# A planner for TensorE's tiles and a VectorE-GpSimd exclusion, a new order of parts, and key products of two heads in turn, in a hybrid encoder block

## Chip, cores and metric

One core of a Trainium2 chip runs the whole kernel. The metric is device time in microseconds (us), from the start of the execution to its end on that core; lower is better.

## What is computed

One layer of an encoder over 512 tokens of width 1024: `x <- LayerNorm(alpha*x + Mixer(x))`, then `x <- LayerNorm(alpha*x + HierMoE(x))`. All matrix work is in float32 or in a split of float32 into two parts. The change touches the mixer, which is, in short:

```python
h = jnp.einsum('btd,de->bte', x, w_in)
(q_na, k_na, v_na, q_dn, k_dn, v_dn, z_dn, b_f, b_b, a_f, a_b, gate_na, gate_dn) = jnp.split(h, offs, axis=-1)
y_na = neighborhood_attention(q_na, k_na, v_na, na_rpb) @ w_proj_na
y_dn = gated_deltanet_bidir(q_dn, k_dn, v_dn, z_dn, ...) @ w_proj_dn
merged = jax.nn.sigmoid(gate_na) * y_na + jax.nn.sigmoid(gate_dn) * y_dn
return merged @ w_out
```

Neighbourhood attention has 8 heads of 64. The gated DeltaNet has 8 heads of 64 and two directions; for each it forms the products of keys with keys and queries, solves a triangular system for each chunk, and scans the chunks with a state of 64 x 64 for each head.

```python
kk = jnp.einsum('bhnid,bhnjd->bhnij', kb, k) * decay
sol = lax.linalg.triangular_solve(a_mat, rhs, left_side=True, lower=True, unit_diagonal=True)
intra = jnp.einsum('bhnid,bhnjd->bhnij', q, k) * decay
def step(S, xs):
    v_new = u_c - jnp.einsum('bhik,bhkv->bhiv', w_c, S)
    o = jnp.einsum('bhik,bhkv->bhiv', qe, S) + jnp.einsum('bhij,bhjv->bhiv', a_c, v_new)
    S = S * jnp.exp(gl)[..., None, None] + jnp.einsum('bhik,bhiv->bhkv', ke, v_new)
```

## The kernel before

The program has three stretches. The first, the mixer with the first LayerNorm and the router, is recorded and then ordered by a planner (`Plan`): each operation goes into a list with its engine (V is VectorE, DVE in the profile; S is ScalarE, ACT; G is GpSimd, POOL; PE is TensorE; Y is the DMA queue of SyncE, SP), a cost from `Plan.cost`, and the operations that it must follow. `Plan.emit` ranks each operation by the longest chain of costs behind it, plays the engines forward with these costs, takes the best-ranked operation that can start, and writes the instructions out in that order. Each engine then runs its own instructions strictly in that order. The second stretch is the mixture of experts (written out by hand, 17 rounds), the third the last LayerNorm, ordered by the same planner.

What the mixer is made of, by the names that appear in the rows:

- `dense` makes one 128-column slice of `h`: 8 pieces of weights are loaded (`wraw`), split into two parts (ACT writes `whi`, POOL `wlo`), and 24 matmuls of 512 columns (`mm<-xhi,whi`, `mm<-xlo,whi`, `mm<-xhi,wlo`) add up in PSUM. There are 44 such slices and one narrow one. They wait for little and serve as filler for everything else. `K`, `Q` and `V` slices feed the DeltaNet and pass a convolution on DVE (`cy`), `Z` slices its output gate, `G` slices the 16 merge gates, and `q` and `v` steps make the slices of neighbourhood attention.
- `D` steps (`delta_step`) are the DeltaNet of four heads, `D00` to `D03` for the first four and `D10` to `D13` for the others. `products` makes the decay (`psp<-Gh,mfr`, `E`) and the key products: four matmuls per call, in each 64 rows of one head against 256 columns (`psp<-kqv`), whose results go through the one PSUM buffer `psp` and are multiplied by `E` on DVE into `NA`. There are 8 calls. `solve` inverts a triangular matrix by doubling: for each of 6 levels four short matmuls (`ps<-RR,N` or `ps<-RR,NT`), a copy to SBUF (`ylv`, on DVE or ACT), eight short matmuls (`ps<-ylv,RR`, `ps<-RR,ylv`) and an update (`RR`, on DVE or ACT). `scan` carries the state on (`vn`, `S`, `O`), and `rms` ends the four heads (`osq`, `zs`).
- `s` steps (`na_scores`) and `o` steps (`na_out`) are the attention of two heads: 8 score matmuls with 64 rows (`psn<-kqv`, 64 or 128 columns), softmax on DVE, ACT and POOL, transposes (`psn<-con,sb`), and 8 output matmuls, each of 64 output rows (`psn<-PT,kqv`). There are 64 of each kind in all.

A matmul with 64 rows or 64 output rows uses half of TensorE's 128 x 128 array, and the instruction says which half. In the profile such a matmul has the form `64*128`, `128*64` or `64*64`, all others `128*128`; a float32 matmul appears as two MATMUL rows, so `x2` is one of them.

`SEQ` lists the parts in the order in which they are recorded. Ties of rank and the order in which PSUM and SBUF buffers are given out follow it. `+a4`, `+b6` and `+d6` open buffers for gates, `+c -c` and `+n -n` the work space of the convolution and of attention.

The planner before costs a matmul by its columns alone, plus a weight load when the matmul ahead is too short to hide it; it knows no cost for going from the full array to half of it and back, and it lets DVE and POOL run side by side at all times.

Of the kernel before, what the change touches and what calls it, by code (L numbers as in the profile page):

```python
# [9 lines left out]
F32 = mybir.dt.float32  # L10
# [67 lines left out]
"""  # L78


# [3 lines left out]

NORM1 = "VGV VGV VGV VGV VVG VVG SGV SVG".split()
NORM2 = "VSGG QD QSGG QPS QSGV QSGV QPS QD A B A B".split()


class Ref:
# [73 lines left out]


class Op:
    __slots__ = ("eng", "call", "args", "kw", "cost", "pred", "succ", "rank", "bytes", "pool", "prio", "cover", "at")

    def __init__(self, eng, call=None, args=(), kw=None):
        self.eng, self.call, self.args, self.kw = eng, call, args, kw or {}
        self.cost, self.pred, self.succ, self.rank, self.bytes, self.pool = 0.0, set(), [], 0.0, 0, None  # L170
        self.prio = self.cover = self.at = 0.0


class Stack:
# [16 lines left out]
class Plan:  # L191
# [57 lines left out]
    def record(self, eng, name, args, kw):  # L249
        op = Op(eng, name, args, kw)  # L250
        op.prio = self.prio
        out = [kw["out"]] if "out" in kw else [args[0]]
        out += [kw["accum_out"]] if "accum_out" in kw else []
        refs = [(r, False) for r in list(args) + list(kw.values()) if isinstance(r, Ref) and not any(r is o for o in out)]
        refs += [(r, True) for r in out if isinstance(r, Ref)]
        for r, wr in refs:
            t = r.tile
            box = (0, 127, 0, t.size) if t.pool.psum else r.box()
            for o, b in t.writes + (t.reads if wr else []):
                if o is not op and b[0] <= box[1] and box[0] <= b[1] and b[2] <= box[3] and box[2] <= b[3]:  # L260
# [17 lines left out]
        return op  # L278

    def cost(self, eng, name, args, kw, out):  # L280
        if eng == "Y":
# [3 lines left out]
        if eng == "PE":  # L285
            dt = args[1].view.dtype
            if name == "transpose":
                return 0.003 + max(args[1].shape[0], 64) * (2 if dt == F32 else 1) / 2400
            if dt == F32:
                return 0.003 + max(4 * n / 2400, 0.16)  # L290
            return 0.003 + max(n, 64) / 2400
        if name in ("tensor_reduce", "bn_stats"):
            return 0.07 + int(np.prod(args[1].shape[1:])) / 960
        if name == "reciprocal":
            return 0.07 + n / 160
        psum = any(r.tile.pool.psum for r in ins)
        if eng == "S":
            extra = 0.09 * sum(isinstance(kw.get(k), Ref) for k in ("bias", "scale", "accum_out"))
            return (0.05 if psum else 0.09) + n / 1200 + extra
        if eng == "G":  # L300
            if name == "memset":
                return 0.035 + n / 1200
            if name == "affine_select":
                return 0.06 + n / 960
            return 0.15 + n / (480 if ins[-1].view.dtype == F32 and len(ins) > 2 else 600)
        if self.ptr and name in ("tensor_scalar", "scalar_tensor_tensor"):
            n += 58 * sum(isinstance(r, Ref) for r in args[2:4 if name == "tensor_scalar" else 3])
        fast = not psum and (all(r.view.dtype == F16 for r in ins) or len(ins) == 2)
        return 0.07 + n / (1920 if fast else 960)

    def emit(self, wait=WAIT, trace=True):
# [20 lines left out]
            if not left[o]:  # L332
                cand[o.eng].append(o)
        order, dma, self.when = [], 0.0, []
        pe = 1.0

        def start(o):
            if o.eng == "PE":
                load = 0.03 if o.args[1].view.dtype == F16 else 0.107
                return max(free["PE"] + max(0.0, load - pe), est[o])  # L340
            return max(free[o.eng], est[o])

        for _ in range(len(ops)):
            best = None
            for k, c in cand.items():
                if not c:
                    continue
                m = min(max(free[k], est[o]) for o in c) + wait.get(k, 0)
                if k == "PE":
                    o = max((o for o in c if est[o] <= m),  # L350
                            key=lambda o: o.rank + o.prio - LAM * max(0.0, LOADT[o.args[1].view.dtype == F16] - pe))
                else:
                    o = max((o for o in c if est[o] <= m), key=lambda o: o.rank + o.prio)
# [6 lines left out]
            if o.eng is not None:  # L360
                free[o.eng] = end
            if o.eng == "PE":
                pe = o.cover
# [59 lines left out]
def encoder_block(ctx, tc, aps, out):  # L423
# [4 lines left out]
    pool = plan.pool  # L428
# [274 lines left out]
    def products(gr, t):  # L703
# [4 lines left out]
            NAs.append(un.tile([128, 2, 4, 128], F32, name="NAl" if late else "NA", bufs=3 if late else 2))  # L708
        kq = KQT[gr]
        tt = slice(t * 128, t * 128 + 128)  # L710
        for h in range(2):
            kp = ps([128, 2, 2, 128], tag="p")
            r = slice(h * 64, h * 64 + 64)
            for p in range(2):
                PE.matmul(kp[:, p], kq[r, p, 0, tt], kq[r, p, :, tt], start=True, stop=True,
                          skip_group_check=True)
            for d in range(2):
                V.tensor_tensor(NAs[d][:, :, h::2], kp.rearrange("p a q i -> p q a i"),
                                Es[d][:, None, h::2].to_broadcast([128, 2, 2, 128]), op=OP.mult)
        return NAs  # L720

# [1178 lines left out]
```

## Time and profile before

| | us |
|---|---|
| median of 3 runs | 981.56 |
| lowest, highest | 974.43, 985.82 |
| profiled execution, whole | 980.33 |
| its span, first to last instruction | 978.5 |
| TensorE busy in the span | 919.2 |
| VectorE busy | 529.9 |
| GpSimd busy | 361.6 |
| ScalarE busy | 357.3 |

The profiled execution took 1.8 us more than its span and stands 1.2 us under the median. Busy time of PE is the union of modelled pipeline times: a PE that is busy all the time need not be issuing at its peak, so the starts of its rows say more than their lengths. The mixer up to the output projections takes the first half of the span (its first projection starts at 515.7 us), the rest of the planned stretch goes to about 640 us, the experts to about 965 us.

### The profile page before, as it was taken

How to read it: one execution, taken by the hardware profiler on the slowest of the kernel's cores; microseconds unless marked ns; L12 is line 12 of the kernel's file. 1: busy time of each engine (PE TensorE's matmuls, PEld its weight loads, DVE VectorE, ACT ScalarE, POOL GpSimd, SP SyncE). 2: the span in 40 equal slices, each digit the busy share in tenths (PEclk: the TensorE clock that was granted, in tenths of full speed). 3: DMA queues.
4: the chain of work that ended last, by engine and by line, in shares of the span. 5: the costliest groups of instructions: out<-in, count | busy, mean ns of one | idle time of the engine just before them, and what ended most of it. 6: DMA issues, size and time to landing. Idle time of an engine off the chain costs nothing. (4 is left out here: it accounts for less than half of the span.)

```text
span 978.5 us, 15388 instructions
## 1 busy us (share of the span) xinstructions
PE 919.2 (94%) x5667; PEld 593.4 (61%) x5667; DVE 529.9 (54%) x1181; ACT 357.3 (37%) x925; POOL 361.6 (37%) x500
## 2 busy tenths in 40 slices
PE   7899989999999999999999999779999999999995
PEld 5666766776677666677788789753343343343432
DVE  5889887649743352330322337844455454455447
ACT  5455554435645564444353321202112121121114
POOL 5766446447545433444556742410000000001003
PEclk9999979999999999999999999889999999999997
DMA  6220000121021221111246455949998999999402
GB/s 238 66 65 22 24 22 23 45 70 44 23 66 44 71 72 44 49 45 44 86 172 222 145 222 208 381 179 330 344 344 308 374 357 357 324 378 368 185 1 86
DMA packets 39965, 157.71 MB, mean 161 GB/s; under 512 B 5786, under 2 KB 6042, under 8 KB 29008
## 3 DMA queue, kind: packets, MB, share of 16 engines
q1 hardware_dynamic: 37584, 152.81, 43.3%
q0 software_dynamic: 2304, 3.90, 1.2%
q8 instruction: 45, 0.74, 0.3%
q14 instruction: 32, 0.26, 0.1%
HBM read 156.99 MB, written 4.19 MB: 165 GB/s over the span
## 5 line engine op out<-in xcount | busy, mean ns | idle before, releaser
L392 POOL TENSOR_TENSOR wlo<-wraw,whi 128x256 fp32r<-128x256 f32 (+1 forms) x220 | 162.9, 753 | 169.1 <-ACT whi L392 114.6
L392 PE MATMUL mm<-xhi,whi 128*128 128x512 f32 (+1 forms) x360 | 142.9, 431 | 13.8 <-ACT whi L392 4.8
L392 PE MATMUL mm<-xhi,wlo 128*128 128x512 f32 (+1 forms) x360 | 142.0, 426 | 0.0
L392 PE MATMUL mm<-xlo,whi 128*128 128x512 f32 (+1 forms) x360 | 140.8, 424 | 0.0
L1591 PE MATMUL hp<-wu,xT 128*64 128x512 f32 x544 | 137.4, 607 | 0.0
L1565 DVE TENSOR_TENSOR xn<-xn,gat 128x512 f32<-128x512 f32 x128 | 86.6, 686 | 89.0 <-PE gat L1563 89.0
L392 ACT CAST whi<-wraw 128x256 fp32r<-128x256 f32 (+1 forms) x228 | 87.4, 405 | 129.5 <-PE mm L392 83.9
L1563 PE MATMUL gat<-part,hot 128*128 128x512 f32 x256 | 92.8, 444 | 0.0
L392 PEld LDWEIGHTS mm<-xhi,whi 128*128 128x128 f32 (+1 forms) x360 | 66.8, 192 | 33.0 <-issue 9.8
L1563 PEld LDWEIGHTS gat<-part,hot 128*128 128x128 f32 x256 | 38.4, 189 | 66.6 <-issue 51.9
L392 PEld LDWEIGHTS mm<-xlo,whi 128*128 128x128 f32 (+1 forms) x360 | 67.0, 191 | 13.5 <-issue 3.2
L392 PEld LDWEIGHTS mm<-xhi,wlo 128*128 128x128 f32 (+1 forms) x360 | 67.0, 191 | 13.4 <-issue 3.5
L1597 ACT ACTIVATE hid<-hp 128x256 f32<-128x256 f32 x17 | 6.5, 385 | 175.3 <-PE hp L1591 175.3
L1591 PEld LDWEIGHTS hp<-wu,xT 128*64 128x64 f32 x544 | 31.7, 135 | 60.3 <-issue 58.0
L1612 PE MATMUL yp<-wu,hid 128*64 128x512 f32 x272 | 62.1, 598 | 0.5 <-ACT hid L1606 0.5
L1577 POOL TENSOR_TENSOR cw<-ic 128x1 f32<-128x1 f32 x17 | 3.2, 187 | 150.3 <-ACT ic L1515 140.7
L392 DVE TENSOR_TENSOR RR<-RR,ps 128x512 f16<-128x512 f16 x64 | 43.1, 682 | 28.7 <-PE ps L392 28.5
L1538 POOL DMA_INDIRECT xg<-x1d,ix x16 | 16.9, 1053 | 111.1 <-DVE oh L1527 92.4
L1556 DVE TENSOR_TENSOR part<-yp,part 128x512 fp32r<-128x512 f32 x34 | 23.4, 692 | 37.0 <-ACT part L1555 37.0
L392 DVE TENSOR_TENSOR ylv<-ps,mlv 128x256 f16<-128x256 f32 x64 | 26.6, 419 | 29.6 <-PE ps L392 29.3
L1612 PEld LDWEIGHTS yp<-wu,hid 128*64 128x64 f32 x272 | 18.0, 136 | 35.8 <-issue 28.8
L1555 ACT CAST part<-yp 128x512 fp32r<-128x512 f32 x34 | 19.8, 586 | 46.7 <-PE yp L1612 45.5
(373 smaller groups left out, 1792.4 us busy)
## 6 DMA issues: line engine op xcount, KB each, us to landing
wu<-in_wgu SPq DMA_DIRECT2D x54, 1024.0 KB, 6.7
wu<-in_wdn SPq DMA_DIRECT2D x28, 1024.0 KB, 6.5
wraw<-in_wT SPq DMA_DIRECT2D x42, 512.0 KB, 3.4
wu<-in_wgu SPq DMA_DIRECT2D x56, 256.0 KB, 5.6
wu<-in_wdn SPq DMA_DIRECT2D x24, 256.0 KB, 5.9
wraw<-in_wp SPq DMA_DIRECT2D x8, 512.0 KB, 3.6
wraw<-in_wo SPq DMA_DIRECT2D x8, 512.0 KB, 3.6
kqv<-in_rpb SPq DMA_DIRECT2D x4, 640.0 KB, 3.9
```

The source lines that it names most:

```text
L392: getattr(self.eng[o.eng], o.call)(*[f(v) for v in o.args], **{k: f(v) for k, v in o.kw.items()})
L1538: G.indirect_dma_start(out=dst, out_offset=None, in_=x1d, in_offset=bass.IndirectOffsetOnAxis(ap=ix, axis=0), bounds_check=T - 1, oob_is_e ...
L1555: S.copy(part[:, c], yps[c])
L1556: V.tensor_tensor(part[:, 2 + c], yps[c], part[:, c].bitcast(F32), op=OP.subtract)
L1563: PE.matmul(sm_, hot[:, t * 128:t * 128 + 128], part[:, 2 * i + h], start=i == 0, stop=i == 1)
L1565: V.tensor_tensor(v, v, sm_, op=OP.add)
L1577: G.tensor_tensor(cw[j], ic[j][:, 0:1], ic[j][:, 1:2], op=OP.add)
L1591: PE.matmul(hp[rows2[h]], xT[:, k, rows2[h]], gw(j, h, k), start=k == 0, stop=k == KC - 1, skip_group_check=True)
L1597: S.activation(hid, hp[:, 0:256], AF.Tanh, scale=0.5)
L1612: PE.matmul(y[rows2[h]], hT[:, f, rows2[h]], dw(j, h, f, c), start=f == 0, stop=f == 1, skip_group_check=True)
```

## The change

Six edits: five in what orders the mixer, one in how it issues a product.

1. `SEQ` has another order of parts: the first value slice and a `Z` slice come ahead, `Q` slices come earlier, all four `Z` slices and four gates stand among the DeltaNet's parts in other places, `D10` comes ahead of the end of the convolutions' work space, the steps of attention among `D11` to `D13` change places, and 7 gates instead of 6 stand behind `+d6`.
2. The planner models TensorE by a class `Array`: the mode (which part of the array), a group (which half), a weight load per group that is not hidden behind the same group, two parts for a float32 matmul, and 0.095 us (`DRAIN`) for each change of mode.
3. The choice among ready PE operations is by rank minus `LAM` (10, was 20) times the time that the array would stand still for it.
4. Operations of POOL and those of DVE that read and write SBUF alone exclude each other in the planner (`port`).
5. An operation of PE that follows one of PE may start when that one starts.
6. `products` takes two PSUM buffers, `psn` for one half's heads and `ps0` for the other's, and issues the four matmuls in turn between the halves; before it issued both of one half, then both of the other, through `psp`.

```diff
 WAIT = {"PE": 0.05, "V": 0.1, "S": 0.1, "G": 0.2, "Y": 0.0, None: 0.0}
-LAM = 20.0
-LOADT = (0.107, 0.03)
+LAM = 10.0
+DRAIN = 0.095
 SEQ = """
-+a4 +c K00 Q00 V00 K01 Q01 V01 D00 K10 K11 D01 Q10 Q11 Z0 D02 V10 V11 Z1 G G G G D03 Z2 Z3 -c +n D10
-q0 v0 s00 s01 q1 o00 o01 v1 s10 s11 D11 q2 o10 o11 v2 s20 s21 D12 q3 o20 o21 v3 s30 s31 D13 o30 o31
--n +b6 G G G G G G -m +d6 G G G G G G
++a4 +c V00 K00 Z0 Q00 K01 Q10 Q01 V01 D00 K10 D01 Z1 Q11 D02 K11 V11 G V10 G G D03 D10 G Z2 Z3 -c +n
+q0 s00 v0 s01 o00 o01 q1 v1 s11 s10 D11 q2 o10 o11 v2 s21 o21 D12 s20 o20 q3 v3 s30 s31 D13 o30 o31
+-n +b6 G G G G G -m +d6 G G G G G G G
 """
+class Array:
...
+    def run(self, o, est, commit=False):
+        mode, group, load, part, parts = o.array
+        issue, f, tk = self.issue, 0.0, 0.0
+        if mode == self.mode:
+            f, tk = self.free.get(group, 0.0), self.taken.get(group, 0.0)
+        elif self.mode is not None:
+            issue = max(issue, self.end() + DRAIN)
+        first = None
+        for _ in range(parts):
+            st = max(max(issue, tk, est) + load, f, issue + 0.007)
+            first = st if first is None else first
+            issue = tk = st
+            f = st + part
...
+        op.port = eng == "G" or eng == "V" and self.shared(name, args, kw, out[0])
         if eng == "PE":
-            op.cover = int(np.prod(out[0].shape[1:])) / (1200 if args[1].view.dtype == F32 else 2400)
+            op.array = self.array(name, args)
+            op.cost = op.array[4] * max(op.array[2], op.array[3])
...
         def start(o):
             if o.eng == "PE":
-                load = 0.03 if o.args[1].view.dtype == F16 else 0.107
-                return max(free["PE"] + max(0.0, load - pe), est[o])
-            return max(free[o.eng], est[o])
+                return pe.run(o, est[o])[0]
+            s = max(free[o.eng], est[o])
+            if o.port:
+                s = max(s, port["V" if o.eng == "G" else "G"])
+            return s
+
+        def gain(o):
+            return o.rank + o.prio - LAM * (pe.run(o, est[o])[0] - max(pe.end(), est[o]))
...
-                est[q] = max(est[q], end + self.lat(o, q))
+                est[q] = max(est[q], s if o.eng == q.eng == "PE" else end + self.lat(o, q))
...
+        kp = [ps([128, 2, 2, 128], tag="n0"[h]) for h in range(2)]
+        for p in range(2):
+            for h in range(2):
+                r = slice(h * 64, h * 64 + 64)
+                PE.matmul(kp[h][:, p], kq[r, p, 0, tt], kq[r, p, :, tt], start=True, stop=True,
+                          skip_group_check=True)
         for h in range(2):
-            kp = ps([128, 2, 2, 128], tag="p")
-            r = slice(h * 64, h * 64 + 64)
-            for p in range(2):
-                PE.matmul(kp[:, p], kq[r, p, 0, tt], kq[r, p, :, tt], start=True, stop=True,
-                          skip_group_check=True)
```

The instructions are the same in kind and number on each engine; their order changes on all of them. Three places show it.

On PE, in the output of attention (`psn<-PT,kqv`), before, between dense matmuls (`mm`):

```order
L392 MATMUL mm<-xhi,whi 128x512 x2
L392 MATMUL mm<-xlo,whi 128x512 x2
L392 MATMUL psn<-PT,kqv 64x128
L392 MATMUL mm<-xhi,wlo 128x512 x2
L392 MATMUL psn<-PT,kqv 64x128
L392 MATMUL mm<-xhi,whi 128x512 x2
L392 MATMUL psn<-PT,kqv 64x128
```

The same place now, the first output matmuls of the same two heads:

```order
L447 MATMUL mm<-xhi,whi 128x512
L447 MATMUL mm<-xlo,whi 128x512 x2
L447 MATMUL mm<-xhi,wlo 128x512
L447 MATMUL mm<-xhi,whi 128x512
L447 MATMUL mm<-xhi,wlo 128x512
L447 MATMUL mm<-xlo,whi 128x512
L447 MATMUL psn<-PT,kqv 64x128 x8
```

The eight output matmuls, which stood one by one between pairs of dense ones, stand together.

On PE, the key products of the last four heads (`psp<-kqv 128x256`, before), among dense and score matmuls:

```order
L392 MATMUL mm<-xlo,whi 128x512
L392 MATMUL mm<-xhi,wlo 128x512
L392 MATMUL mm<-xhi,whi 128x512
L392 MATMUL psp<-kqv 128x256
L392 MATMUL mm<-xlo,whi 128x512
L392 MATMUL psn<-kqv 128x128
L392 MATMUL mm<-xhi,wlo 128x512
L392 MATMUL psn<-kqv 128x128 x2
L392 MATMUL psp<-kqv 128x256
```

The key products of the last four heads now, where `psn` holds one half's and `ps_2852` the other's:

```order
L447 MATMUL mm<-xlo,whi 128x512
L447 MATMUL pss<-vn,NAl 128x64 x4
L447 MATMUL psn<-kqv 128x256
L447 MATMUL ps_2852<-kqv 128x256
L447 MATMUL psn<-kqv 128x256
L447 MATMUL ps_2852<-kqv 128x256
L447 MATMUL pss<-S_327,kqv 128x128 x4
```

One call of the four now stands in one piece and in turn between the halves; in the first four heads the two halves of a call still stand apart for the most part, two matmuls at one place and two at another.

On SP, the loads of the dense slices' weights (`wraw<-in_wT`) and of attention's bias (`kqv<-in_rpb`, one ahead of each pair of heads), before:

```order
L392 DMA conb<-in_conb 128x1280
L392 DMA wraw<-in_wT 128x1024 x17
L392 DMA kqv<-in_rpb 128x1280
L392 DMA wraw<-in_wT 128x1024 x8
L392 DMA kqv<-in_rpb 128x1280
L392 DMA wraw<-in_wT 128x1024 x4
L392 DMA kqv<-in_rpb 128x1280
L392 DMA wraw<-in_wT 128x1024 x3
L392 DMA kqv<-in_rpb 128x1280
L392 DMA wraw<-in_wT 128x1024 x10
```

The same loads now:

```order
L447 DMA conb<-in_conb 128x1280
L447 DMA wraw<-in_wT 128x1024 x23
L447 DMA kqv<-in_rpb 128x1280
L447 DMA wraw<-in_wT 128x1024 x3
L447 DMA kqv<-in_rpb 128x1280
L447 DMA wraw<-in_wT 128x1024 x2
L447 DMA kqv<-in_rpb 128x1280
L447 DMA wraw<-in_wT 128x1024 x4
L447 DMA kqv<-in_rpb 128x1280
L447 DMA wraw<-in_wT 128x1024 x10
```

Six slices have moved from between the bias loads to ahead of the first one (23 and 17), so 9 stand between the four bias loads where 15 stood.

## Rows read from the trace of the kernel before

**Rows 1.** The page, part 2: busy tenths in 40 equal slices of the span.
```profile
PE   7899989999999999999999999779999999999995
PEclk9999979999999999999999999889999999999997
```

**Rows 2.** Stretches: length; PE, PEld, DVE, ACT, POOL busy us (instructions); clock; DMA; GB/s.
```profile
45.00:300.00 255.00, 235.89 (x2059) 179.40 (x2059) 188.72 (x394) 127.24 (x329) 141.71 (x186) 0.96 0.13 42
300.00:470.00 170.00, 169.09 (x1094) 116.85 (x1093) 55.12 (x143) 86.61 (x255) 75.26 (x118) 1.00 0.16 54
```

**Rows 3.** Timeline, PE, attention's output: start us, us, engine, line, operation, tiles, form, xcount.
```profile
326.07 0.43 PE L392 MATMUL psn<-PT,kqv 128*64 128x128 f32 x2
326.43 0.73 PE L392 MATMUL mm<-xhi,wlo 128*128 128x512 f32 x2
327.10 0.43 PE L392 MATMUL psn<-PT,kqv 128*64 128x128 f32 x2
```

**Rows 4.** Timeline, PE, dense matmuls alone, late in the mixer.
```profile
493.84 0.62 PE L392 MATMUL mm<-xlo,whi 128*128 128x512 f32 x2
494.30 0.62 PE L392 MATMUL mm<-xhi,wlo 128*128 128x512 f32 x2
```

**Rows 5.** Timeline, PE, six output matmuls that stand together.
```profile
441.34 1.38 PE L392 MATMUL psn<-PT,kqv 128*64 128x128 f32 x12
442.65 0.88 PE L392 MATMUL pss<-x,NAl 128*128 128x64 f32 x6
```

**Rows 6.** Timeline, PE, key products: one matmul, then two of the same half.
```profile
87.96 0.70 PE L392 MATMUL psp<-kqv 64*128 64x256 f32 x2
88.59 0.29 PE L392 MATMUL ps<-ylv,RR 128*128 128x64 f16 x4
...
90.62 1.13 PE L392 MATMUL psp<-kqv 64*128 64x256 f32 x4
91.68 0.29 PE L392 MATMUL ps<-RR,N 128*128 128x64 f16 x4
```

**Rows 7.** The page, part 5: key products on their way through DVE.
```profile
L392 DVE TENSOR_TENSOR NA<-psp,E 128x512 f32<-128x512 f32 x20 | 13.5, 686 | 5.0 <-PE psp L392 4.1 <-PE pss L392 0.9
```

**Rows 8.** Timeline, PE and DVE, one level of a solve.
```profile
165.04 0.28 PE L392 MATMUL ps<-RR,ylv 128*128 128x64 f16 x4
...
165.36 0.69 DVE L392 TENSOR_TENSOR RR<-RR,ps 128x512 f16<-128x512 f16 x1
...
166.43 0.29 PE L392 MATMUL ps<-RR,NT 128*128 128x64 f16 x4
...
166.75 0.42 DVE L392 TENSOR_TENSOR ylv<-ps,mlv 128x256 f16<-128x256 f32 x1
...
167.56 0.29 PE L392 MATMUL ps<-ylv,RR 128*128 128x64 f16 x4
```

**Rows 9.** Timeline, PE, a stretch of the first four heads without dense matmuls (those between left out).
```profile
120.20 0.39 PE L392 MATMUL mm<-xhi,wlo 128*128 128x512 f32 x1
...
128.60 1.22 PE L392 MATMUL psp<-kqv 64*128 64x256 f32 x2 [0.38 <-ACT E L392]
...
134.30 0.77 PE L392 MATMUL mm<-xhi,whi 128*128 128x512 f32 x1
```

**Rows 10.** The four stretches up to 300 us at clock 0.50: the longest, their sum.
```profile
127.80:138.00 10.20, 9.29 (x69) 6.06 (x68) 6.91 (x17) 3.44 (x11) 4.08 (x6) 0.50 0.17 51
...
sum 20.40, PE 19.50 PEld 14.11 DVE 13.62 ACT 6.75 POOL 10.14; mean PE 4.87 PEld 3.53 DVE 3.41 ACT 1.69 POOL 2.53
```

**Rows 11.** Instructions by tile (min/median/max ns, first and last start): solve, scan and end of the DeltaNet.
```profile
L392 ACT COPY NT<-psp x16: 1002/1012/1039, 75.4 to 351.3; 128x1024 f16<-128x1024 f16 x16
L392 ACT COPY vn<-pss x16: 358/373/413, 103.5 to 464.0; 128x256 f32<-128x256 f32 x16
L392 ACT COPY vn<-pss x4: 372/373/375, 181.8 to 205.5; 128x256 f32<-128x256 f32 x4
L392 DVE SCALAR_TENSOR_TENSOR zs<-pss,nw,zs x4: 742/748/750, 230.9 to 493.1; 128x512 f32<-128x512 f32 x4
```

More of the change, by code (lines that the diff above doesn't have):

```diff
@@ L86, with __init__, end @@
 NORM2 = "VSGG QD QSGG QPS QSGV QSGV QPS QD A B A B".split()
+class Array:
+    def __init__(self):
+        self.mode, self.free, self.taken, self.issue = None, {}, {}, 0.0
+    def end(self):
+        return max(self.free.values(), default=0.0)
+    def run(self, o, est, commit=False):
[11 more added lines that the diff above has]
+            f = st + part
+        if commit:
+            if mode != self.mode:
+                self.mode, self.free, self.taken = mode, {}, {}
+            self.free[group], self.taken[group], self.issue = f, tk, issue
+        return first, f
 class Ref:
@@ L165 @@
 class Op:
-    __slots__ = ("eng", "call", "args", "kw", "cost", "pred", "succ", "rank", "bytes", "pool", "prio", "cover", "at")
+    __slots__ = ("eng", "call", "args", "kw", "cost", "pred", "succ", "rank", "bytes", "pool", "prio", "array", "at", "port")
     def __init__(self, eng, call=None, args=(), kw=None):
@@ L170, in __init__ @@
         self.cost, self.pred, self.succ, self.rank, self.bytes, self.pool = 0.0, set(), [], 0.0, 0, None
-        self.prio = self.cover = self.at = 0.0
+        self.prio = self.at = 0.0
+        self.array, self.port = None, False
 class Stack:
@@ L278, in record, with shared, array @@
         return op
+    def shared(self, name, args, kw, out):
+        ins = [r for r in list(args[1:]) + list(kw.values()) if isinstance(r, Ref) and int(np.prod(r.shape[1:])) > 1]
+        ins = [r for r in ins if r is not out]
+        if out.tile.pool.psum or any(r.tile.pool.psum for r in ins):
+            return False
+        if name in ("tensor_tensor", "scalar_tensor_tensor"):
+            return True
+        return name in ("tensor_scalar", "tensor_copy", "memset")
+    def array(self, name, args):
+        out, w = args[0], args[1]
+        n = int(np.prod((args[2] if name != "transpose" else out).shape[1:]))
+        K, M = w.shape[0], int(np.prod(w.shape[1:]))
+        size = [32 if x <= 32 else 64 if x <= 64 else 128 for x in (K, M)]
+        at = (w.box()[0] // size[0] if size[0] < 128 else 0, out.box()[0] // size[1] if size[1] < 128 else 0)
+        dt = w.view.dtype
+        load = M * (1 if dt == F16 else 4) / 4800
+        if name == "transpose":
+            return tuple(size), at, load, n / 2400, 1
+        if dt == F32:
+            return tuple(size), at, load, n / 1200, 2
+        return tuple(size), at, load, n / 2400 + (0.005 if dt == F16 else 0.01), 1
     def cost(self, eng, name, args, kw, out):
-        if eng == "Y":
+        if eng in ("Y", "PE"):
             return 0.06
@@ L284, in cost @@
         ins = [r for r in list(args) + list(kw.values()) if isinstance(r, Ref)]
[L285 to L291, printed above, removed]
         if name in ("tensor_reduce", "bn_stats"):
@@ L334, in emit @@
         order, dma, self.when = [], 0.0, []
-        pe = 1.0
+        pe, port = Array(), {"V": 0.0, "G": 0.0}
         def start(o):
             if o.eng == "PE":
-                load = 0.03 if o.args[1].view.dtype == F16 else 0.107
-                return max(free["PE"] + max(0.0, load - pe), est[o])
-            return max(free[o.eng], est[o])
+                return pe.run(o, est[o])[0]
[5 more added lines that the diff above has]
+            return o.rank + o.prio - LAM * (pe.run(o, est[o])[0] - max(pe.end(), est[o]))
         for _ in range(len(ops)):
@@ L348, in emit @@
                 m = min(max(free[k], est[o]) for o in c) + wait.get(k, 0)
[L349 to L353, printed above, removed]
+                o = max((o for o in c if est[o] <= m), key=gain if k == "PE" else lambda o: o.rank + o.prio)
                 s = start(o)
@@ L359, in emit @@
             end = s + o.cost
-            if o.eng is not None:
+            if o.eng == "PE":
+                s, end = pe.run(o, est[o], True)
+                free["PE"] = pe.issue
+            elif o.eng is not None:
                 free[o.eng] = end
-            if o.eng == "PE":
-                pe = o.cover
+            if o.port:
+                port[o.eng] = end
             if o.eng == "Y" and o.call != "none":
@@ L710, in products @@
         tt = slice(t * 128, t * 128 + 128)
[L711 to L716 removed]
+        kp = [ps([128, 2, 2, 128], tag="n0"[h]) for h in range(2)]
[4 more added lines that the diff above has]
+                          skip_group_check=True)
+        for h in range(2):
             for d in range(2):
[L718 removed]
+                V.tensor_tensor(NAs[d][:, :, h::2], kp[h].rearrange("p a q i -> p q a i"),
                                 Es[d][:, None, h::2].to_broadcast([128, 2, 2, 128]), op=OP.mult)
```

## The prediction

> **What bounds the kernel now.** I read the slices first, then the stretches, then the timeline of TensorE (PE) inside them. The slices [rows 1] show PE at 9 tenths or more almost everywhere, with dips at the very start, in slices two to five and near the router. The stretches [rows 2] divide the mixer: from 45 to 300 us, where the DeltaNet of the first four heads runs, PE is busy 235.89 of 255 us, so 19.1 us idle, while DVE is busy 188.72 (74%). From 300 to 470 us, where attention and the other four heads run, PE is busy 169.09 of 170, and DVE only 55.12. So in the second stretch what PE issues sets the time, in the first one partly what it waits for. The change leaves the instructions of every engine as they are, and the experts' code too; PE is busy there nearly throughout. I cost the experts, projections and LayerNorms at nothing: they follow the mixer and should only shift.
>
> In the second stretch busy does not mean useful. In the timeline [rows 3] a single output matmul of attention starts at 326.07, the next at 327.10, with two dense matmuls between: 1.03 us. Two dense matmuls alone take 0.46 us [rows 4]. So one output matmul costs 0.57 us, of which 0.36 lies between its start and the next dense one (326.07 to 326.43) and 0.21 in the neighbours' starts. Six that stand together take 1.31 us from start to successor [rows 5], with the same 0.21 around them 1.52, or 0.25 each. The difference of 0.32 us is what leaving the full array, coming back, and loading weights that nothing hides costs.
>
> **Output matmuls.** By my count of the order, the 64 stood in 60 pieces: 57 of one, two of two, one of three; without full-array work between them that makes 58 visits. At 56 singles x 0.57 plus 0.6 and 1.5 for the two longer visits this is 34.0 us. Now there are 15 visits: 8 of five to eight matmuls (55 in all, 13.8 us at 0.25), 2 of two (0.57 each, one in each half), 5 of one (2.9): 17.8 us. Gain 16 us, nearly all in the stretch where PE is full, so on the path. Bounds: 8 us, if grouped matmuls gained half of what rows 5 show; 20, if eight in a row cost less than six.
>
> **Key products.** One matmul takes 0.63 us to its successor (87.96 to 88.59), two of one half 1.06 (90.62 to 91.68) [rows 6]; with 0.21 around, 0.84 and 1.27. Before: 16 singles and 8 twos, 23.6 us. Four in turn between halves are not in the trace; the bounds are 1.27 (the halves run fully beside each other) and 2.3 (one after the other). I take 1.27, because the six of rows 5, which also alternate, took 1.31 and not six times a single's 0.36. But the order shows that only 3 of 8 calls got both halves together; the others remain 7 twos, one three and 3 singles. That makes 11 x 1.27 + 3 x 0.84 = 16.5 us: gain 7. The bounds are 3 and 10.
>
> Here a rule speaks against the change. DVE takes 686 ns for each half and direction of a call [rows 7], 2.7 us per call, twice the 1.27 that PE would need. The Trainium skill, "TensorEngine Tiling (Array Packing)", section "PSUM Bottleneck", says that tiling speeds up TensorE but not the evacuation of PSUM, which may then bound. By that the 7 us would be nothing for the solve behind the products. In the second stretch PE has other work meanwhile and DVE is busy a third of the time, so what PE saves counts; I keep the 7.
>
> **Scores and transposes.** The 64 score matmuls stood in 37 visits and stand in 14. At 0.21 around each visit 23 fewer save 4.8 us; now and then three of the same half follow each other, so I take 4 (bounds 0 and 7). Half-width transposes: 1 us (0 and 2). Sum of the regrouping: 16 + 7 + 4 + 1 = 28 us.
>
> **The solves.** One level is two hops. After the last short matmul is issued (three steps of 0.03 us behind 165.04), the update RR runs from 165.36 to 166.05; after that of 166.43, `ylv` runs from 166.75 to 167.17 [rows 8]. With a tenth for the start on PE, PE needs other work for about 1.05 and 0.75 us. I counted in both orders the PE work that stands in these places, at the spacing of rows (0.23 us a dense matmul, 0.03 a short one): of 176 places, 62 hold too little before and 25 now, and what lacks adds up to 11.8 and 5.0 us. Gain 7 us. Bounds: 0, as DVE may be late for other reasons (its 74%), and 19, all the idle time of the first stretch. New PSUM buffers can delay as well: `ps0` also serves the solves of one direction, `psn` the convolutions' transposes, so a product waits for them and they for its two multiplications by E on DVE (2 x 0.69 us); the idle time of PE in the first four heads covers this, as three of these four calls were split because of it.
>
> **The clock.** Four stretches up to 300 us run at clock 0.50, 1.2 instead of 2.4 GHz, 20.4 us in sum [rows 10]; the longest follows a stretch in which PE had only the solves' short matmuls and waits [rows 9], and a key product took 1.22 us there instead of 0.70. At most half of 20.4, 10 us, comes back; I take 3, and 10 in either direction as bounds, since the new order can have its own dips.
>
> **What is moved to where.** Six dense slices are now loaded, and issued, ahead of attention: 6 x 24 x 0.23 = 33 us of filler leave the second stretch for the first. That helps the solves above and starves what comes later. Before, one bare stretch of 115 matmuls lasted from 120.43 to 134.30 [rows 9], where their own steps come to about 6 us: 8 lost, partly by the clock. Now five bare stretches of 50 to 107 matmuls, 353 in all, lie in the second stretch. At the same rate they would lose 25 us, 17 more than now. But attention has longer and independent matmuls there (0.25 us, not 0.03), so I charge 5 (bounds 0 and 17).
>
> **Sum.** 28 + 7 + 3 - 5 = 33 us. The profiled execution took 980.33 us, so 947; it stands 1.2 under the median of 981.56, on whose scale I say 948 us.
>
> **Rivals.**
> A. *The first stretch heals.* If the moved filler takes all of PE's idle time and the clock stays up, the gain is 28 + 19 + 10 = 57: 924 us. For it: the starved places fall to less than half. Against: DVE's 74% does not change.
> B. *Only attention gains.* PE waits on DVE in the first stretch however it is ordered, so the gain there (about 5 of the 7 for key products, the solves, the clock) is nothing, and the bare stretches cost 12: 16 + 2 + 5 - 12 = 11, 970 us. For it: the split calls, and the bare stretches in the order.
> C. *The DeltaNet ends too late (slower).* The last transposes of a solve now have 544 matmuls, 268 of them dense, between them and the first projection; before 791 and 411. At 0.23 us and some 0.08 for the others that is 84 us of work. The chain through solve, scans and `rms` needs 28 us from the first solve's copy (75.4) to its first scan (103.5), 3 scans of 7.9 (181.8 to 205.5), and 29 from the last scan (464.0) to the last `zs` (493.1), 81 in sum; before it took 142 (351.3 to 493.1) [rows 11]. If it still takes 142, PE waits 58: 980 - 33 + 58 = 1005 us on the profiled scale, 1006 on the median's. It decides from 84 + 33 = 117 us on.
> D. *It does not do what it says.* If halves do not run beside each other in the longer groups, outputs and key products give 11, not 23: 960 us.
>
> **Chances.** The forecast 0.56, A 0.14, B 0.14, D 0.06, no change to be told (gains given back to bare stretches, clock and PSUM waits, about 977) 0.05, C 0.05. A difference of 1%, 10 us, is about what a measurement of this kernel can tell from no change; 971.7 is that bound. B lies at it, so half of it and a little of the forecast's tail (0.01) count as the same. Faster 0.82, same 0.13, slower 0.05. The range leaves C, the no-change case and the better half of A out: 924 to 972.
>
> **What would show it.** Right: output matmuls as x8 to x16 rows instead of x2, about 18 us of the second stretch in them; PE idle in the first stretch under 19 us; the first projection some 33 us earlier; from there to the end the same length as now. Wrong: PE rows with waits on ACT or DVE in the bare stretches, waits of `projd` on `zs`, new stretches at clock 0.50, or key products that stay at 1.06 us for two while four take 2.

## The result and the profile after

The changed kernel takes 935.1 us (median of 4 runs, 933.1 to 935.8) against 981.2 for the kernel before: ratio 0.953, 95% interval 0.947 to 0.959, a gain of 46 us where 33 were forecast. The time lies inside the range of 924 to 972.

The instructions by tile (min/median/max ns, first and last start) show where the gain ends:

```profile
L447 PE MATMUL projn<-yhn,whi x32: 389/389/389, 471.2 to 515.4; 128*128 128x512 f32 x32
...
L447 ACT COPY NT<-psp x16: 1012/1012/1016, 85.7 to 378.0; 128x1024 f16<-128x1024 f16 x16
...
L447 DVE TENSOR_TENSOR NA<-psn,E x10: 672/679/692, 77.4 to 372.3; 128x512 f32<-128x512 f32 x10
...
L447 DVE SCALAR_TENSOR_TENSOR zs<-pss,nw,zs x4: 743/750/752, 300.4 to 451.1; 128x512 f32<-128x512 f32 x4
```

The first projection starts at 471.2 us instead of 515.7, 44.5 us earlier. From there to the end of the span it is 934.0 - 471.2 = 462.8 us, and 978.5 - 515.7 = 462.8 before: what lies behind the mixer only shifts. The last `zs` is done 19 us before the first projection, so the DeltaNet does not end too late; from its last `NT` copy to its last `zs` it now takes 73 us (378.0 to 451.1), before 142 [rows 11].

The slices, which answer to [rows 1]:

```profile
PE   7999999999999999999999997799999999999994
...
PEclk9999999999989997999999999899999999999997
```

The stretches (length; PE, PEld, DVE, ACT, POOL busy; clock; DMA; GB/s), which answer to [rows 2] and [rows 10]:

```profile
0.00:45.00 45.00, 39.26 (x164) 28.95 (x165) 31.69 (x61) 21.28 (x50) 29.55 (x53) 0.99 0.50 167
45.00:300.00 255.00, 246.50 (x1984) 191.40 (x1983) 163.23 (x383) 140.91 (x370) 155.26 (x207) 0.98 0.17 56
300.00:470.00 170.00, 164.24 (x1350) 132.55 (x1349) 87.43 (x199) 92.92 (x262) 88.51 (x127) 0.97 0.18 60
...
351.21:361.45 10.24, 9.39 (x66) 9.02 (x66) 3.76 (x9) 4.86 (x15) 4.12 (x6) 0.50 0.14 52
sum 23.90, PE 23.05 PEld 20.45 DVE 11.67 ACT 12.85 POOL 10.08; mean PE 5.76 PEld 5.11 DVE 2.92 ACT 3.21 POOL 2.52
```

The first 45 us and the sum to 470 us in the kernel before, which [rows 2] leave out:

```profile
0.00:45.00 45.00, 34.47 (x149) 25.45 (x149) 30.50 (x70) 21.65 (x53) 27.27 (x49) 1.00 0.46 154
...
sum 470.00, PE 439.45 PEld 321.71 DVE 274.35 ACT 235.51 POOL 244.24; mean PE 146.48 PEld 107.24 DVE 91.45 ACT 78.50 POOL 81.41
```

Three things are to be seen. PE's idle time fell from 10.5 to 5.7 us in the first 45 and from 19.1 to 8.5 from there to 300 us; from 300 to 470 us it rose from 0.9 to 5.8. DVE lost 25 us of work in the first stretch (188.72 to 163.23, a share of 64% instead of 74%) and gained 32 in the second. And the four stretches at clock 0.50 last 23.9 us, not less than the 20.4 before.

The timeline of PE in four places of the mixer's second half, which answer to [rows 3, 5, 6, 9], and the forms of the output matmuls:

```profile
257.67 0.39 PE L447 MATMUL mm<-xlo,whi 128*128 128x512 f32 x1
257.99 1.39 PE L447 MATMUL psn<-PT,kqv 128*64 128x128 f32 x16
259.32 0.29 PE L447 MATMUL ps<-ylv,RR 128*128 128x64 f16 x4
...
321.69 0.48 PE L447 MATMUL ps<-kqv 64*128 64x256 f32 x1
321.75 0.48 PE L447 MATMUL psn<-kqv 64*128 64x256 f32 x1
...
322.81 0.29 PE L447 MATMUL ps<-RR,N 128*128 128x64 f16 x4
...
324.87 0.88 PE L447 MATMUL psn<-PT,kqv 128*64 128x128 f32 x12
325.72 0.28 PE L447 MATMUL ps<-RR,N 128*128 128x64 f16 x4
...
348.36 1.39 PE L447 MATMUL psn<-PT,kqv 128*64 128x128 f32 x16
352.06 0.37 PE L447 MATMUL ps<-RR,NT 128*128 128x64 f16 x4 [2.31 <-ACT RR L447]
...
361.63 0.48 PE L447 MATMUL psp<-Gh,mfr 128*128 128x512 f32 x1
...
L447 PE MATMUL psn<-PT,kqv x128: 269/273/324, 258.0 to 403.5; 128*64 128x128 f32 x96, 64*64 64x128 f32 x32
```

Eight output matmuls take 1.33 us to their successor and 0.09 at their start (257.67 to 257.99 less the 0.23 of a dense matmul): 0.18 each, where a single cost 0.57 and six in a row 0.25. Part of that last difference is form: a timeline row prints its first form alone, but a quarter of the output matmuls are `64*64`. The six at 324.87 are all `128*64`, in pairs of both halves, and take 0.88 us. The six of [rows 5] had two of `64*64` among them, their first and last had none of the other half beside them, and they took 1.38. Four key products take 1.12 us, two of one half took 1.06. The place at 348.36 is one of the bare stretches: no dense matmul stands between 348 and 361.6 us, PE waits 2.3 us for an `RR`, and in that wait the clock falls to 0.50 for 10 us.

What PE spends on half of the array can be added up from the starts in both traces: for each such row the time to the start of the next row, less idle time, and for the dense matmuls beside them what they take beyond 0.23 us. Up to the first projection, in us:

| | before | changed |
|---|---|---|
| output matmuls | 31.9 | 12.6 |
| key products | 21.4 | 14.9 |
| scores | 21.6 | 15.5 |
| half-width transposes | 4.3 | 4.1 |

### The profile page after: what moved, and what is told of

It reads as the page before. It is cut to its first block, busy times and chain, and to the rows that moved or that the text cites. A ratio compares the mean times of both kernels' runs of the same rounds, so it can differ in the third digit from the quotient of the medians.

```text
span 934.0 us, 15388 instructions
## 1 busy us (share of the span) xinstructions
PE 885.5 (95%) x5667; PEld 589.0 (63%) x5667; DVE 525.8 (56%) x1181; ACT 356.8 (38%) x925; POOL 364.3 (39%) x500
## 5 line engine op out<-in xcount | busy, mean ns | idle before, releaser
L447 POOL TENSOR_TENSOR wlo<-wraw,whi 128x256 fp32r<-128x256 f32 (+1 forms) x220 | 165.2, 764 | 150.0 <-ACT whi L447 110.4
L447 PE MATMUL mm<-xhi,whi 128*128 128x512 f32 (+1 forms) x360 | 140.3, 416 | 8.1 <-ACT whi L447 4.8
L447 PE MATMUL mm<-xhi,wlo 128*128 128x512 f32 (+1 forms) x360 | 139.2, 411 | 0.0
L447 PE MATMUL mm<-xlo,whi 128*128 128x512 f32 (+1 forms) x360 | 138.0, 410 | 0.1
L1647 PEld LDWEIGHTS hp<-wu,xT 128*64 128x64 f32 x544 | 31.7, 135 | 60.3 <-issue 57.7
L1611 ACT CAST part<-yp 128x512 fp32r<-128x512 f32 x34 | 19.8, 586 | 47.1 <-PE yp L1668 45.9
```

The costliest lines, as they stand in the source:

```text
L447: getattr(self.eng[o.eng], o.call)(*[f(v) for v in o.args], **{k: f(v) for k, v in o.kw.items()})
L1611: S.copy(part[:, c], yps[c])
L1647: PE.matmul(hp[rows2[h]], xT[:, k, rows2[h]], gw(j, h, k), start=k == 0, stop=k == KC - 1, skip_group_check=True)
```

## Experiments

Each run stands against runs of the kernel before on the same chip. "First projection" is the start of the first `projn` matmul, "PE idle" is 470 us less PE's busy time from 0 to 470 us, and "at 0.50" the time up to the first projection that runs at clock 0.50, all of one profiled execution. That of "before, new order of parts" took 985.8 us, 9 above its median, so its last three columns say little; the others lie within 3.3 us of their medians, those of "no exclusion" and "no mode change priced" 2.8 and 2.3 above.

| run | us | ratio to before, 95% | first projection | PE idle | at 0.50 |
|---|---|---|---|---|---|
| before | 981.2 | | 515.7 | 30.6 | 20.4 |
| changed kernel | 935.1 | 0.953 (0.947 to 0.959) | 471.2 | 20.0 | 23.9 |
| changed, order of parts of before | 951.9 | 0.971 (0.968 to 0.973) | 485.8 | 29.2 | 34.1 |
| changed, no mode change priced | 951.5 | 0.969 (0.965 to 0.972) | 488.3 | 24.6 | 20.5 |
| changed, no exclusion | 947.5 | 0.965 (0.963 to 0.967) | 483.6 | 30.0 | 30.7 |
| changed, products of before | 947.3 | 0.965 (0.963 to 0.967) | 481.4 | 26.5 | 23.9 |
| changed, `LAM` 20 | 942.7 | 0.960 (0.957 to 0.963) | 478.2 | 25.1 | 23.9 |
| changed, `DRAIN` 0.1 | 937.4 | 0.955 (0.951 to 0.958) | 474.6 | 20.9 | 23.9 |
| changed, `LAM` 11 | 935.9 | 0.956 (0.952 to 0.959) | 466.6 | 19.8 | 13.6 |
| changed, halves one after the other | 936.1 | 0.954 (0.951 to 0.957) | 471.8 | 20.2 | 23.9 |
| changed, output matmuls apart | 948.9 | 0.967 (0.964 to 0.971) | 484.0 | 21.0 | 13.6 |
| before, new order of parts | 976.6 | 0.997 (0.995 to 0.999) | 519.3 | 31.4 | 30.7 |
| before, new products | 980.8 | 0.999 (0.996 to 1.003) | 517.3 | 26.4 | 30.7 |
| before, exclusion alone | 989.4 | 1.011 (1.007 to 1.015) | 523.6 | 31.6 | 34.1 |

At half the clock a stretch loses at most half its length, so where "at 0.50" differs by 10 us between two runs, up to 5 us of the difference in time can be the clock.

**The order of parts, taken back and alone.** In the first run the changed kernel gets the `SEQ` of before, in the second the kernel before gets the new one:

```diff
 SEQ = """
-+a4 +c V00 K00 Z0 Q00 K01 Q10 Q01 V01 D00 K10 D01 Z1 Q11 D02 K11 V11 G V10 G G D03 D10 G Z2 Z3 -c +n
...
++a4 +c K00 Q00 V00 K01 Q01 V01 D00 K10 K11 D01 Q10 Q11 Z0 D02 V10 V11 Z1 G G G G D03 Z2 Z3 -c +n D10
...
```

> The changed kernel with the order of parts of the kernel before; planner and key products as changed. Theory 1 (most of the 46 us comes from grouping the half-array matmuls and from pricing the array, whatever the order of parts): 53 visits to half the array as against 56, so the regrouping's 28 us stay and what goes is the part of the filler; 945 to 955 us. Theory 2 (the order of parts carries most, since it brings six dense slices to the first stretch): 960 to 970 us. If the order of parts is worth nothing by itself: 935 us.

> The kernel before with the new order of parts alone; old planner, old key products. 133 visits instead of 143. Theory 1: 965 to 978 us, PE still 94% busy and the output matmuls still one by one. Theory 2: 945 to 955 us. If old planner and new order do not fit together: over 981 us.

Measured: 951.9 and 976.6 us, both as theory 1 had it. Alone the new order of parts is worth 4 us, in the changed kernel 17, of which up to 5.1 can be the clock (34.1 us at 0.50 instead of 23.9); the rest of the change without it is worth 29. Of the 14.6 us by which the first projection is later in the first run, 9.2 are idle time of PE: 8.3 us in the first 45 (changed kernel 5.7), 13.7 from 45 to 300 (8.5), 7.2 from there to 470 (5.8):

```profile
0.00:45.00 45.00, 36.73 (x151) 26.52 (x152) 29.66 (x66) 22.14 (x53) 30.61 (x53) 0.93 0.49 165
45.00:300.00 255.00, 241.27 (x1904) 186.16 (x1902) 164.39 (x370) 136.26 (x354) 146.37 (x198) 0.97 0.16 52
```

So planner and products carry most of the gain, and the order of parts pays little without them.

**The price of a mode change, taken out of the planner.**

```diff
-        elif self.mode is not None:
-            issue = max(issue, self.end() + DRAIN)
+        else:
+            f, tk = self.end(), self.taken.get(group, 0.0)
```

> The changed kernel whose planner charges nothing for a change of mode and hides weight loads behind any matmul; the exclusion, the order of parts and the key products as changed. 106 visits instead of 56. Theory 1 (grouping is the largest part): 50 visits more at 0.32 us or a little over are 16 to 20 us, so 950 to 957 us, nearly all of the loss between 250 and 430 us. Rival (the filler carries most, and PE's model matters little): 935 to 943 us.

The edit also lets the planner hide a weight load behind any matmul. Measured: 951.5 us, 16 more than the changed kernel. The first projection is 17.1 us later; PE is idle for 4.6 of them and busy for 12.5. Added up from the starts as above, 9.8 of the 12.5 lie on half of the array and at the dense matmuls beside it: outputs 5.0, scores 4.1, key products 0.9, transposes 0.2 less. That fits a price paid in leaving and entering half the array. But planning anew moves everything else too; the next experiment avoids that.

**Output matmuls apart, with the order kept.** Behind the planner, dense matmuls that were free to run are moved forward between the output matmuls of a group:

```diff
+def apart(order):
...
+        for o in pe[j:j + 60]:
+            if of(o, 1, "whi") or of(o, 1, "wlo"):
+                if o in taken or any(at.get(q, -1) > at[pe[i]] and q not in free for q in o.pred):
+                    break
+                free.append(o)
...
+        for o, q in zip(pe[i:j], free):
+            after[o] = q
...
-        self.span = max(w[1] for w in self.when)
+        order = apart(order); self.span = max(w[1] for w in self.when)
```

> The order of the changed kernel is kept, but behind its planner 37 dense matmuls are moved forward so that 40 of the 64 output matmuls of attention, which stood in groups, stand alone between dense matmuls again; nothing is planned anew. Theory 1, the grouping itself pays: each of the 40 costs 0.57 us instead of 0.18 (the x16 rows of the changed kernel, 1.42 us for eight), +15.6 us, so 949 to 952, and the rows of output matmuls are x2 again. Theory 2, the grouping is only a by-product and the gain comes from fewer waits in a better order: under +5, 935 to 940, with PE idle as before at about 20 us.

In the order as it ran, 34 dense matmuls have moved, not 37, and 40 output matmuls that stood in groups stand alone. Measured: 948.9 us, 13.8 more. The timeline of PE in this run, at the first group of eight:

```profile
259.01 0.43 PE L447 MATMUL psn<-PT,kqv 128*64 128x128 f32 x2
259.37 0.50 PE L447 MATMUL mm<-xhi,wlo 128*128 128x512 f32 x1
259.80 0.43 PE L447 MATMUL psn<-PT,kqv 128*64 128x128 f32 x2
...
264.53 0.43 PE L447 MATMUL psn<-PT,kqv 128*64 128x128 f32 x2
264.89 0.29 PE L447 MATMUL ps<-ylv,RR 128*128 128x64 f16 x4
```

From one single to the next it is 0.79 us, less 0.23 for the dense matmul 0.56: the price of [rows 3, 4], now with everything else in place. Eight take 264.89 - 259.01 - 7 x 0.23 = 4.27 us against 1.33 together (257.99 to 259.32), 0.37 more each; 40 x 0.37 = 14.8, and 13.8 were measured. PE's idle time stays (21.0 and 20.0 us), so grouping pays directly, and a better order as the only cause is refuted. The agreement is not as close as it looks: this run has 13.6 us at clock 0.50 instead of 23.9, which can hide some 5 us, so the 40 may be worth up to 19.

**The key products, taken back and alone.** The first run gives the changed kernel the products of before (one buffer, `psp`), the second gives the kernel before the new ones:

```diff
-        kp = [ps([128, 2, 2, 128], tag="n0"[h]) for h in range(2)]
-        for p in range(2):
-            for h in range(2):
...
         for h in range(2):
+            kp = ps([128, 2, 2, 128], tag="p")
...
```

> The changed kernel with the key products as before: one half, then the other, through the one buffer psp. Order of parts and planner as changed. 63 visits instead of 56, 21 with key products instead of 14. Theory 1: 7 visits at about 0.5 us more, 937 to 943 us. Rival (two PSUM buffers and the turns are what lets the solves run ahead): 950 us or more. Rival (the buffers ps0 and psn are in the way of solves and transposes): 925 to 933 us.

> The kernel before with the key products as changed alone (two PSUM buffers, in turn between the halves); old planner, old order of parts. 146 visits instead of 143; the old planner spreads the output matmuls as before and takes a call's products apart again. Theory 1 (the edit pays only where the planner holds the four together): 976 to 984 us. Rival (two buffers let the solves start earlier whatever the planner): 965 to 972 us.

Measured: 947.3 us, 12 more than the changed kernel and between what theory 1 and its rival had, and 980.8, no difference. In the first, the key products stand in 21 visits to half the array instead of 14 and take, added up as above, 20.8 us instead of 14.9; PE is idle 6.5 us longer and waits for ACT to empty the one buffer that products, decay and transposes share (the waits of PE up to 481 us: in total, times, longest), and DVE is at 74% in the first stretch again:

```profile
PE psp L447 <- ACT E L447: 2.8, 2, 1.5
...
PE psp L447 <- ACT NT L447: 0.8, 1, 0.8
```

```profile
45.00:300.00 255.00, 239.69 (x2070) 183.46 (x2070) 188.92 (x410) 137.51 (x354) 152.30 (x199) 0.95 0.15 47
```

And by tile, in this run:

```profile
L447 DVE TENSOR_TENSOR NA<-psp,E x20: 674/682/693, 76.5 to 318.0; 128x512 f32<-128x512 f32 x20
```

The last product is multiplied by `E` at 318 us here (319.5 in the kernel before), in the changed kernel at 372 to 373: with two buffers of their own the planner lays the products of the last four heads later, and their solves with them, from the crowded stretch into the one where DVE had room. The second run shows that this alone gains nothing. There DVE's work moves in the same way:

```profile
45.00:300.00 255.00, 239.62 (x1834) 179.26 (x1833) 158.19 (x356) 131.29 (x343) 139.57 (x189) 0.99 0.16 52
```

PE is idle 4.2 us less than in the kernel before, but up to the first projection it is busy 490.3 us instead of 485.1, with 30.7 us at clock 0.50 instead of 20.4: key products and outputs stand as far apart as before (20.6 and 32.8 us, added up as above).

**Halves one after the other, with the order kept.** Whether taking turns matters was asked directly. At the three calls whose four products stand in one piece, the two of one half are put ahead of the two of the other:

```diff
-L447 MATMUL ps_4457<-kqv 128x256
-L447 MATMUL psn<-kqv 128x256
-L447 MATMUL ps_4457<-kqv 128x256
-L447 MATMUL psn<-kqv 128x256
+L447 MATMUL ps_4457<-kqv 128x256 x2
+L447 MATMUL psn<-kqv 128x256 x2
```

> The order of the changed kernel is kept to the instruction, only at the three calls whose four key products stand in one piece the two of one half now stand ahead of the two of the other, in the same two buffers. Theory 1, issuing in turn is what the edit of the products is worth: at most 3 x (2.3 - 1.27) = 3.1 us, so 938, and each of the three rows grows from 1.2 to about 2.3 us. Theory 2, what the edit is worth (12 us when it is undone and planned anew) is the separate PSUM buffers, which no longer share the one of the decay and the transposes: 935 to 936.

Measured: 936.1 us, no difference that can be told. The timeline of PE shows why, at the call whose diff stands above (issued `ps`, `ps`, `psn`, `psn`; each is two rows):

```profile
322.21 0.48 PE L447 MATMUL ps<-kqv 64*128 64x256 f32 x1
322.27 0.48 PE L447 MATMUL psn<-kqv 64*128 64x256 f32 x1
322.53 0.38 PE L447 MATMUL ps<-kqv 64*128 64x256 f32 x1
322.59 0.38 PE L447 MATMUL psn<-kqv 64*128 64x256 f32 x1
...
323.33 0.29 PE L447 MATMUL ps<-RR,N 128*128 128x64 f16 x4
```

The halves run beside each other all the same, 1.12 us for four. So taking turns is worth nothing, and what the edit is worth comes with the buffers: before, the second half's products could not be issued until DVE had emptied the one that the first half's had filled, and so the four could not stand together. Whether it is the second buffer or that neither is the one of decay and transposes was not told apart.

**The exclusion, taken out and alone.** The first run drops the line from the changed planner; the second adds it, and its two uses in `start` and behind the choice, to the planner of before:

```diff
-        op.port = eng == "G" or eng == "V" and self.shared(name, args, kw, out[0])
```

> The changed kernel without the planner's exclusion of VectorE and GpSimd; all else as changed. 57 visits, nearly the same order of dense matmuls on PE. Theory 1: within 1% of the changed kernel, 932 to 944 us, since PE bounds the mixer. Rival (the exclusion makes the planner's starts true and that is what fills PE): 945 to 960 us.

> The kernel before, with its order of parts, its costs of matmuls and its products; only the exclusion of GpSimd and of VectorE operations within SBUF is added to its planner. Theory 1, the exclusion pays by itself as it does in the changed kernel (12 us when taken out): 968 to 972, with PE idle in the mixer under 25 us. Theory 2, it pays only where the planner also knows what TensorE loses, since before the changes of array mode cover what VectorE is late by: 977 to 983.

Measured: 947.5 us, 12 more than the changed kernel and in the rival's range, and 989.4, 10 more than before. What is modelled is plain in the timeline of DVE and POOL of the changed kernel (rows of other engines left out):

```profile
50.98 0.15 DVE L447 TENSOR_TENSOR cr_t<-cr_h 128x8 f32<-128x8 f32 x1
...
51.07 0.74 POOL L447 TENSOR_TENSOR wlo<-wraw,whi 128x256 fp32r<-128x256 f32 x1 [0.64 <-ACT whi L447]
51.17 0.66 DVE L447 SCALAR_TENSOR_TENSOR cr_t<-cr_t,css 128x8 f32<-128x8 f32 x1
...
51.86 0.17 DVE L447 SCALAR_TENSOR_TENSOR cr_h<-cr_t,cr_h 128x8 f32<-128x8 f32 x1
```

A DVE operation of 8 columns takes 0.15 to 0.17 us, and 0.66 while POOL's `wlo` runs, until 51.81. The Trainium skill, "SBUF — State Buffer", section "Terms", says of the port pair that DVE and GpSimd share that it is held for a whole instruction and the loser blocks; these rows agree. Without the exclusion in the planner, PE's idle time from 45 to 300 us is 19.0 us, that of the kernel before, though DVE is busy no longer than in the changed kernel (63 and 64%). Up to 3.4 of the 12 us can be the clock (30.7 us at 0.50). PE waits for operations that come late:

```profile
45.00:300.00 255.00, 235.99 (x1861) 182.16 (x1859) 161.63 (x370) 135.29 (x353) 144.97 (x195) 0.96 0.16 51
```

```profile
PE psn L446 <- DVE sb L446: 3.0, 1, 3.0
PE psp L446 <- ACT N L446: 2.3, 1, 2.3
```

Added alone to the kernel before, it costs 10 us, against both expectations: PE is idle as long as before, and the stretches at clock 0.50 grow from 20.4 to 34.1 us, 13.7 more at half speed, which by itself costs at most 6.9:

```profile
40.12:53.78 13.66, 11.50 (x37) 9.43 (x38) 8.35 (x29) 5.97 (x17) 8.13 (x10) 0.50 0.03 14
...
sum 34.14, PE 27.83 PEld 22.27 DVE 23.44 ACT 13.21 POOL 15.27; mean PE 6.96 PEld 5.57 DVE 5.86 ACT 3.30 POOL 3.82
```

**The weight of standstill, and two controls.** `LAM` 20 as before, and, to see how much a planner's answer moves by chance, `DRAIN` 0.1 for 0.095 and `LAM` 11 for 10:

```diff
-LAM = 10.0
+LAM = 20.0
```

> The changed kernel with LAM 20 instead of 10: 49 visits instead of 56, the output matmuls in eights. Theory 1 if more grouping is still a gain: 930 to 935 us. Rival (what the grouping holds back is later missed as waits in the bare stretches): 940 to 950 us.

> A control: the changed kernel with DRAIN 0.100 instead of 0.095, 5 ns in the planner, nothing else; 61 visits instead of 56. If the planner's result is stable: 932 to 938 us, and differences of 12 us between the kernels with one edit undone are the edits' own. If the planner's order jumps with any small change: anything up to 950 us, and the 12 us each of the undone exclusion and the undone turns are partly the loss of one good order.

> A second control: the changed kernel with the weight of standstill at 11 instead of 10, which moves a few of the choices only. If the planner's answer is stable, and the differences of single edits mean what they say, the time stays within 3 us of the changed kernel, 932 to 938; if small shifts of the order are worth as much as the edits, it moves by 8 or more.

Measured: 942.7, 937.4 and 935.9 us. The two small shifts move the time by 0.8 and 2.3 us, so the 12 to 17 us of the edits lie well above what a small shift did here, while `LAM`'s 7.5 is not far above it. With `LAM` 20 the time lies in the rival's range: there are fewer visits, 49 instead of 56, and PE is idle 25.1 us instead of 20.0. Undone one at a time, the edits are worth 16.7 (order of parts), 16.4 (mode changes), 12.4 (exclusion) and 12.2 us (products), 57.7 in sum, more than the whole gain of 46, also less the 8.5 us that can be the clock (5.1 in the order of parts, 3.4 in the exclusion): they need each other. No run has a median under that of the changed kernel.

## Why the prediction was right, and where it was not

The mechanism that bore the forecast was right: fewer visits to half the array, at the price that single visits had. The sum was 11.5 us too low at the first projection (33 against 44.5), mostly for what it left out: the start, the exclusion, and how little eight outputs together cost.

An account of the 44.5 us from the stretches: PE's idle time fell by 30.6 - 20.0 = 10.6 us, so 33.9 us are time in which PE was busy. The forecast had 31 for the busy part (28 and 3 for the clock) and 2 for the idle part (7 less 5). Of the 33.9 us, 32.1 lie on half of the array and at the dense matmuls beside it, where 28 were summed; the other 1.8 were not divided.

- **Output matmuls (16 us): right, somewhat small.** They took 31.9 us before and 12.6 now, 19.3 us less, where the sum had 34.0 and 17.8. Eight in a row cost 0.18 us each, less than the 0.25 taken; the upper bound of 20 had foreseen that. The singles' 0.57 was 0.56 when the order was kept. That halves would not run beside each other (rival D) is refuted by 1.33 us for eight, and by two halves' key products that start 0.06 us apart.
- **Key products (7 us): the size right, the turns not needed.** They took 21.4 and now 14.9 us, 6.5 less. The prediction took 1.27 us for four because they alternate, with 2.3 as the bound one after the other. Four cost 1.12 us in turn and 1.12 one half after the other: what counts is that both halves' products stand together, and the buffers allow that. The Trainium skill, "TensorEngine Tiling (Array Packing)", section "PSUM Bottleneck", was the rule weighed against this term. By it the term would have been nothing, and it was not. Where the products share one buffer again, the trace agrees with its direction: PE waits 3.6 us for ACT to empty `psp`, and in the changed kernel no wait of `psp` is in the list.
- **Scores and transposes (5 us): right.** Scores took 21.6 and 15.5 us, 6.1 less where 4 were taken, half-width transposes 4.3 and 4.1, 0.2 less where 1 was taken. No run tests them by themselves.
- **The solves (7 us): mis-sized, and its cause incomplete.** The idle time from 45 to 300 us fell by 10.6 us, within the bounds of 0 to 19. "DVE's 74% does not change", which spoke against rival A, did not hold: it became 64%, since the products of the last four heads moved behind 300 us. But a lighter DVE is not enough: without the exclusion it is at 63% and with the buffers alone at 62%, and PE's idle time there is 19.0 and 15.4 us. The exclusion was given no price at all; without it these 10.6 us are back. The count of starved places knew neither.
- **The start, costed at nothing:** PE's idle time in the first 45 us fell by 39.26 - 34.47 = 4.8 us, which the prediction had no term for. With the old order of parts 2.5 of them are lost, and the new order alone has them (5.0 us idle in the first 45, in an execution above its median).
- **The clock (3 us): wrong in sign, inside its bounds.** 23.9 us at 0.50 instead of 20.4, at most 1.7 us lost. The new dip that the bounds allowed for is there, at 351 us.
- **The bare stretches (-5 us): right.** The idle time behind 300 us rose by 5.8 - 0.9 = 4.9 us, and the longest wait, 2.3 us, stands in a bare stretch.
- **Rivals.** A (924 us) came half true, 10.6 of 19 us of idle time, without the clock. B (970) had nothing gained in the first stretch, where 10.6 and 4.8 us were. C (1006) needed 142 us for a chain that took 73: how long it took before was how long it was given, not how long it needed.

What stays open: how much of what the single edits are worth is the clock, whose stretches at 0.50 moved with every order (13.6 to 34.1 us); which property of the new buffers counts; and why the exclusion alone leads to longer stretches at 0.50.

## What to carry to other kernels

Where an engine is busy all the time, look at the spacing of its starts: half-array matmuls among full ones cost 0.56 us each here and 0.18 when eight stood together, and a scheduler that knows this price finds the groups by itself. Before crediting an edit with what its text says, keep the order and undo that one thing: issuing in turn was worth nothing, and the buffers that came with it, taken back, cost 12 us. Edits of a planner's model need not pay alone; the exclusion cost 10 us by itself and was worth 12 with the others.

## What the runs showed of the hardware that was not expected

Key products issued as two of one half and then two of the other start 0.06 us apart (322.21 and 322.27) and take 1.12 us, as those issued in turn: with two PSUM buffers PE started the other half's first matmul ahead of the second one of the first half, though it was issued behind it. The section on the kernel before has each engine run its own instructions strictly in the order written; by these starts that does not hold between PE's two halves.

Output matmuls that stand together pay for a change of form among them: six of `128*64` take 0.88 us (324.87), eight with two of `64*64` among them 1.39 (257.99), where 0.88 x 8 / 6 would be 1.17.

In a stretch of short matmuls the clock fell to 0.50 at 351.21 us, within a wait of PE of 2.3 us that ended at 352.06, and stayed there for 10.2 us. From 300 to 470 us PE was busy 164 of 170.
